# Layer 0: the softmax denominators divide the head outputs instead of the probabilities

## The chip, the cores and the metric

The kernel runs on one core of a Trainium2 chip. Its time is the device time of one execution in microseconds (us). The kernel before took 1253.75 us, the median of 3 runs (1253.59 to 1255.1).

The engines are named as the profile names them: PE is the matrix engine (PEld its weight loads), DVE the vector engine, ACT the scalar engine, POOL GpSimd, and SP the engine whose queue issues every DMA of this kernel. SBUF is the memory on the core, PSUM the matrix engine's result memory, DRAM the memory outside.

## The reference

Two layers over 1024 tokens of width 1024, with a final norm. Layer 0 has three groups of heads of width 64, all from one projection: A (6 heads, a window of 128 tokens on each side, a bias and a sink), B (6 heads, dense, with normalised and rotated q and k) and X (4 heads, attention to 256 memory tokens). Cut to what the change touches:

```python
def windowed_gqa_sink(q, k, v, sink, table):        # A
    ...
    sink_col = jnp.broadcast_to(sink.astype(jnp.float32).reshape(1, 1, KVH, G, 1, 1),
                                logits.shape[:-1] + (1,))
    p = jax.nn.softmax(jnp.concatenate([logits, sink_col], axis=-1), axis=-1)[..., :-1]
    out = jnp.einsum("bnkgqs,bnskd->bnqkgd", p.astype(v.dtype), vw)
...
    s = jnp.einsum("bqkgd,bskd->bkgqs", qi, k).astype(jnp.float32) * (D ** -0.5)     # B
    p = jax.nn.softmax(s, axis=-1)
    return jnp.einsum("bkgqs,bskd->bqkgd", p.astype(v.dtype), v)
...
def even_layer(x, ...):                              # layer 0
    y = jnp.concatenate([y_a.reshape(Bn, S, -1), y_b.reshape(Bn, S, -1),
                         y_x.reshape(Bn, S, -1)], axis=-1) * jax.nn.silu(gate)
    return x + y @ w_out
```

Layer 1 has the same shape with 6 differential heads (each the difference of two softmaxes, 128 wide) and 4 X heads; the change leaves its attention alone.

## The kernel before

**Work and its order.** Everything is computed in fp32 split into two parts of a narrower type, a high part (`wh`, `h`, `PTh`) and a low one (`wl`, `PTl`), so one product takes two or three matmuls. A scheduler places the instructions on each engine when the program is built; it fills the matrix engine's time between attention steps with pieces of the projections (line 297, the "jobs"). At run time each engine, and SP with its DMAs, runs its list in that fixed order and waits at each instruction for what it needs.

**An attention step** in layer 0 handles 128 query tokens of a head (B), 256 of a head in two blocks (A), or 128 of all four heads (X). There are 8 X steps, then 8 B steps of head 0, then 40 B and 24 A steps mixed by the string `PAT`. A step has these parts, spread over some five turns of `run_steps`:

1. `s1`: scores into a PSUM tile of tag S, which has two buffers (`sx`, `sb`, `sa`; line 509). DVE takes the minimum `mn` (negated scores), ACT writes `e` = exp and, by accumulation, its row sum `z`. For B a tiny DVE product `mr` = mn times rq (line 1063) stands between. For A, DVE adds the bias and takes the minimum in one instruction (line 1132), and ACT makes the sink's term `es` (line 1139), which DVE adds to `z` (line 1141).
2. `finish`: DVE takes 1/z (lines 596, 1067, 1143) and `e` is multiplied by it: on POOL for B (line 1068) and A (line 1149), on ACT for X (line 598).
3. `hop`, one turn later: a DMA copies `e` to `er`, the type that the matrix engine takes.
4. `s2`, two or three turns after `s1` (`ABLAG` is 3 for the mixed steps): PE transposes `er` into PSUM tiles of tag T, two buffers (`te`, `ta`); ACT writes the high part `PTh` (line 315), DVE the low part `PTl` (line 316), and that frees the T buffer.
5. `s3`, once for two B or X steps and once for an A step: the product with v (`ob`, `oa`, `ox`), in a PSUM tile of tag A, two buffers that the jobs' `acc` share. The high and low halves of v stand in the two halves of the 128 output partitions, so `y_evac` (lines 433 to 439) copies one half with ACT, adds with DVE (`yt`), and POOL multiplies the sum into the gate's tile `gy` at the head's 64 partitions.

When a gate tile is complete it is stored to DRAM (`ysc`). **The output projection** (`out_proj`, after the attention of each layer) goes over 8 token tiles in the order `ORD[l]`. `PRE` says for which tiles a part of the 8 terms was summed during the attention (layer 0: 4 of 8 for tiles 2 to 5, 6 of 8 for 6 and 7; layer 1: 6 of 8 for tiles 2, 3 and 4), so that these tiles are short here: a tile with all terms takes 48 matmuls, with 4 left 24, with 2 left 12. `pieces` gives each tile a buffer of tag S, and the last tile buffers of tag A. The first two tiles in the order begin before the last terms are there. After a tile's matmuls, DVE adds the residual (`x`, line 1274), ACT squares and sums, POOL makes the inverse root (line 229), DVE scales (`xs`, line 1295); in layer 0 PE transposes the result (`tx`, line 344) for layer 1's projections, whose first job needs tokens 0 to 511.

## Time and profile before

| | |
|---|---|
| median of the runs | 1253.75 us (1253.59 to 1255.1) |
| the profiled execution's own time | 1255.58 us |
| its span, first to last instruction | 1253.8 us |
| PE busy in the span | 1205.5 us (96%) |
| DVE, ACT, POOL busy | 817.1, 640.2, 413.5 us |
| mean busy share of the 16 DMA engines | 47.4% (the SP queue) |

By the timeline, layer 0's X steps lie at about 78 to 160 us, its other attention steps up to about 530 us, its output projection from 530 to 597 us, layer 1 after that, and layer 1's output projection from 1184 us to the end. The B steps of head 0 and the mixed steps overlap the projection jobs.

How to read the views: a row of grouped instructions gives line, engine, operation, output<-inputs, shapes, count, then busy us and mean ns, then the idle time of that engine just before these instructions and what ended it. A row of waits gives who waited for whom, total us, times, the longest. A row of windows gives a stretch of the span, its length, and each engine's busy us with its count of instructions, then the granted clock of the matrix engine (1.00 is full), the DMA engines' share and GB/s. Matmuls are pipelined, so PE's "busy" is an upper bound of its work.

### The profile page before, as it was taken

How to read it: one execution, taken by the hardware profiler on the slowest of the kernel's cores; microseconds unless marked ns; L12 is line 12 of the kernel's file. 1: busy time of each engine (PE TensorE's matmuls, PEld its weight loads, DVE VectorE, ACT ScalarE, POOL GpSimd, SP SyncE). 2: the span in 40 equal slices, each digit the busy share in tenths (PEclk: the TensorE clock that was granted, in tenths of full speed). 3: DMA queues.
4: the chain of work that ended last, by engine and by line, in shares of the span. 5: the costliest groups of instructions: out<-in, count | busy, mean ns of one | idle time of the engine just before them, and what ended most of it. 6: DMA issues, size and time to landing. Idle time of an engine off the chain costs nothing. (4 is left out here: it accounts for less than half of the span.)

```text
span 1253.8 us, 19637 instructions
## 1 busy us (share of the span) xinstructions
PE 1205.5 (96%) x6806; PEld 999.2 (80%) x6806; DVE 817.1 (65%) x1545; ACT 640.2 (51%) x1395; POOL 413.5 (33%) x390
## 2 busy tenths in 40 slices
PE   5999999999998999998999999999999999999997
PEld 4887788888887787887888778788887878877876
DVE  5547666377778788746355865766667666678444
ACT  6249654256666766533157644444444454456322
POOL 5023456266666565403122212212122131223100
PEclk9999999999999999999999999999999999999999
DMA  6654444545365575466644334243342433445363
GB/s 252 198 187 149 155 168 150 171 155 201 148 224 191 210 246 186 154 203 213 185 163 144 125 107 120 93 143 108 105 137 76 136 115 118 144 151 189 129 211 118
DMA packets 96350, 199.90 MB, mean 159 GB/s; under 512 B 11478, under 2 KB 31190, under 8 KB 96252
## 3 DMA queue, kind: packets, MB, share of 16 engines
q1 hardware_dynamic: 96252, 198.65, 47.4%
q8 instruction: 54, 0.88, 0.3%
q14 instruction: 44, 0.36, 0.1%
HBM read 79.32 MB, written 31.47 MB: 88 GB/s over the span
## 5 line engine op out<-in xcount | busy, mean ns | idle before, releaser
L297 PE MATMUL acc<-h,wh 128*128 128x512 f32 x1536 | 499.1, 399 | 7.3 <-DVE yt L624 3.1
L297 PEld LDWEIGHTS acc<-h,wh 128*128 128x128 f32 x1536 | 283.2, 188 | 73.3 <-issue 13.4
L297 PE MATMUL acc<-h,wl 128*128 128x512 f32 x768 | 304.6, 397 | 1.8 <-POOL wl L241 1.8
L241 POOL TENSOR_TENSOR wl<-wr,wh 128x512 fp32r<-128x512 f32 x96 | 124.9, 1302 | 340.0 <-DVE wh L239 125.2
L316 DVE TENSOR_TENSOR PTl<-te,PTh 128x512 fp32r<-128x512 f32 x224 | 148.2, 687 | 131.2 <-ACT PTh L315 128.4
L1440 ACT ACTIVATE e<-e,mn 128x1024 f32<-128x1024 f32 x96 | 110.2, 1149 | 130.7 <-DVE mn L1437 127.5
L297 PEld LDWEIGHTS acc<-h,wl 128*128 128x128 f32 x768 | 144.8, 189 | 35.5 <-issue 4.4
L315 ACT CAST PTh<-te 128x512 fp32r<-128x512 f32 x224 | 124.9, 591 | 30.2 <-PE te L540 24.6
L1068 POOL TENSOR_TENSOR e<-e,rz 128x1024 f32<-128x1024 f32 x48 | 91.7, 1913 | 78.1 <-DVE rz L1067 66.7
L1437 DVE CUSTOM_DVE_ANT_0 e<-sc,toep 128x1024 f32<-128x1024 f32 x96 | 113.9, 1217 | 5.3 <-PE sc L1431 5.0
L540 PEld LDWEIGHTS te<-identr,er 128*128 128x128 f32 x896 | 91.8, 143 | 21.1 <-issue 4.1
L540 PE MATMUL te<-identr,er 128*128 128x128 f32 x896 | 100.0, 246 | 7.5 <-issue 3.2
L239 DVE CAST wh<-wr 128x512 fp32r<-128x512 f32 x112 | 59.1, 530 | 43.9 <-PE acc L297 14.4
L1064 ACT ACTIVATE e<-sb,mr,nrq 128x1024 f32<-128x1024 f32 x48 | 58.0, 1208 | 48.4 <-DVE mr L1063 33.9
L1449 DVE SCALAR_TENSOR_TENSOR e<-e,mr 128x1024 f32<-128x1024 f32 x48 | 76.2, 1588 | 1.3
L1464 PE MATMUL oc<-PTh,v 128*128 128x256 f32 x384 | 74.8, 288 | 0.3 <-DVE ckl L1333 0.3
L660 PE MATMUL po<-woh,yh 128*128 128x512 f32 (+1 forms) x172 | 65.9, 383 | 1.5 <-DVE x L1274 1.5
L660 PE MATMUL po<-woh,yl 128*128 128x512 f32 (+1 forms) x172 | 65.6, 381 | 0.0
L660 PE MATMUL po<-wol,yh 128*128 128x512 f32 (+1 forms) x172 | 65.5, 381 | 0.0
L1464 PEld LDWEIGHTS oc<-PTh,v 128*128 128x128 f32 x384 | 61.5, 192 | 0.7 <-DVE ckl L1333 0.6
L1059 DVE TENSOR_REDUCE mn<-sb 128x1 f32<-128x1024 f32 x48 | 58.4, 1216 | 5.1 <-PE sb L509 4.7
L318 ACT ACTIVATE yh<-yr 128x256 fp32r<-128x256 f32 (+2 forms) x56 | 24.0, 448 | 67.3 <-DMA yr<-ysc 38.5
(199 smaller groups left out, 2247.1 us busy)
## 6 DMA issues: line engine op xcount, KB each, us to landing
er<-e SPq DMA_DIRECT2D x112, 512.0 KB, 2.9
wr<-in_w_in SPq DMA_DIRECT2D x96, 256.0 KB, 2.8
ysc<-gy SPq DMA_DIRECT2D x16, 512.0 KB, 2.9
wor<-in_w_out SPq DMA_DIRECT2D x32, 256.0 KB, 3.5
cq<-sg SPq DMA_DIRECT2D x64, 128.0 KB, 2.6
ck<-sg SPq DMA_DIRECT2D x48, 128.0 KB, 2.3
er<-e SPq DMA_DIRECT2D x12, 384.0 KB, 2.8
xpsc<-xh SPq DMA_DIRECT2D x18, 256.0 KB, 2.5
```

The source lines that it names most:

```text
L239: nc.vector.tensor_copy(hi, raw)
L241: (nc.vector if fast else nc.gpsimd).tensor_tensor(out=lo, in0=raw, in1=hi, op=ALU.subtract)
L297: lastmm[0] = nc.tensor.matmul(acc, a, b[:, k, c0:c0 + n], start=(i == 0), stop=(i == 23))
L315: nc.scalar.copy(hi, src)
L316: return nc.vector.tensor_tensor(out=lo, in0=src, in1=hi, op=ALU.subtract)
L540: nc.tensor.transpose(to[:, i * P:(i + 1) * P], e[0][:, k * P:(k + 1) * P], idt)
L660: lastmm[0] = nc.tensor.matmul(acc, a, b, start=(start and n == 0), stop=(stop and n == 2))
L1068: nc.gpsimd.tensor_tensor(out=et, in0=et, in1=rz.to_broadcast([P, 1024]), op=ALU.mult)
L1437: nc.vector.tensor_tensor_reduce(out=et, in0=Sp, in1=toeps[h][:, w0:w0 + 1024], scale=1.0, scalar=BIG, op0=ALU.add, op1=ALU.min, accum_out ...
L1440: nc.scalar.activation(et, et, AF.Exp, bias=mn[:, m:m + 1], scale=-1.0, accum_out=z[:, m:m + 1])
L1449: nc.vector.scalar_tensor_tensor(out=es[0], in0=es[1], scalar=c, in1=es[0], op0=ALU.mult, op1=ALU.add)
L1464: nc.tensor.matmul(acc, V[:, kt, v, :], pt[:, kt, :], start=(n == 0), stop=(n == 23))
```

## The change

- **Layer 0's probabilities stay undivided.** `finish` is gone for all three groups; `e` goes into the copy `er` as exp left it. The row sums of a pair of steps (B: two columns, X: eight) or of an A step (two) are kept in one tile.
- **1/z is spread by two DMAs.** In the hop, `z_rows` takes the reciprocal in place on DVE and a DMA writes it to DRAM with tokens along the row (`rz_d`; 256 single elements for A and B, 1024 for X). In `s2`, `z_tile` issues a second DMA that reads such a row into 64 partitions (`rzb`, 64 x 256, two buffers); X has four of these for a pair.
- **The gate's tile takes the factor.** POOL multiplies `rzb` into `gy` (64 x 256 in `y_evac`, 128 x 256 for X) before it multiplies the head output in.
- **The sink is a score column.** In A, ACT writes the sink's negated score into one more column beside each block's scores, and exp covers it, so that `z` holds it; `es` and its addition go. The copied tile is 769 or 641 columns wide.
- **`mr` moves from DVE to ACT** in the B steps.
- **The output projections** take their tiles in other orders (`ORD`), and the third tile in the order has two PSUM buffers of tag A instead of one of tag S (`pieces`). In both layers two more DVE, ACT and SP instructions come of that third tile's two halves.

Counted over the program, DVE has 94 instructions fewer, POOL 40 fewer, ACT 24 more, SP 118 DMAs more (116 for `rz_d` and `rzb`); PE has as many as before.

DVE at two B steps in the mixed part, before (`sb` are the scores, `wol` a piece of the output weights, `yt` a head output):

```order
L1059 TENSOR_REDUCE mn_4528<-sb_4523 128x1
L258 TENSOR_TENSOR wol_4545<-wor_4608,woh_4544 128x512
L1063 TENSOR_TENSOR mr_4532<-mn_4528,rq_81 128x1
L258 TENSOR_TENSOR wol_4545<-wor_4662,woh_4544 128x512
L438 TENSOR_TENSOR yt_4557<-oa_4550,yt_4557 64x256
L1067 RECIPROCAL rz_4579<-z_4531 128x1
L1059 TENSOR_REDUCE mn_4593<-sb_4588 128x1
L316 TENSOR_TENSOR PTl_4563<-te_4565,PTh_4561 128x4x128
L316 TENSOR_TENSOR PTl_4564<-te_4572,PTh_4562 128x4x128
L1063 TENSOR_TENSOR mr_4597<-mn_4593,rq_81 128x1
```

The same two steps on DVE now:

```order
L1096 TENSOR_REDUCE mn_4501<-sb_4496 128x1
L258 TENSOR_TENSOR wol_4518<-wor_4578,woh_4517 128x512
L439 TENSOR_TENSOR yt_4531<-oa_4523,yt_4531 64x256
L316 TENSOR_TENSOR PTl_4537<-te_4539,PTh_4535 128x4x128
L316 TENSOR_TENSOR PTl_4538<-te_4546,PTh_4536 128x4x128
L1096 TENSOR_REDUCE mn_4564<-sb_4559 128x1
```

`mr` and the reciprocal are gone from between; one reciprocal of both columns follows some rows later.

SP a little later in the mixed part, before (`er` of 1024 columns belong to B steps, of 768 and 640 to A steps; `wor` are output weights):

```order
L175 DMA er_4772<-e_4718 128x1024
L175 DMA wor_4994<-in_w_out0 128x512
L175 DMA er_4823<-e_4781 128x1024
L175 DMA er_4890<-e_4826 128x768
L175 DMA wor_5037<-in_w_out0 128x512
L175 DMA ysc0_94<-gy_3169 128x1024
```

The same steps on SP now:

```order
L175 DMA er_4742<-e_4690 128x1024
L175 DMA yr_4955<-ysc0_94 128x4x128
L175 DMA er_4791<-e_4751 128x1024
L175 DMA rz_d_4794<-es_4691 128x2x1
L175 DMA rz_d_4861<-z2_4799 128x2x1
L175 DMA er_4858<-e_4797 128x769
L175 DMA ysc0_94<-gy_3146 128x1024
L175 DMA wor_4962<-in_w_out0 128x512
L175 DMA rzb_4966<-rz_d_4794 64x256
L175 DMA wor_4982<-in_w_out0 128x512
L175 DMA er_4930<-e_4872 128x1024
```

Each `rzb`, which waits until its `rz_d` has landed, stands some four DMAs behind it, with `er` copies of later steps behind the `rzb`.

DVE in layer 1's output projection, where the first tiles end (`x1` is a tile's sum with the residual, `yl` the low part of a later tile's input), before:

```order
L1274 TENSOR_TENSOR x1_13081<-po_12974,xr_13060 128x1024
L319 SCALAR_TENSOR_TENSOR yl_13135<-yr_13133,yh_13134 128x512
L1274 TENSOR_TENSOR x1_13109<-po_13017,xr_13062 128x1024
L1283 TENSOR_SCALAR v_13086<-z4_13083 128x1
L319 SCALAR_TENSOR_TENSOR yl_13141<-yr_13139,yh_13140 128x256
L1295 SCALAR_TENSOR_TENSOR xs_13082<-x1_13081,r_13088,gb_12936 128x1024
L1283 TENSOR_SCALAR v_13114<-z4_13111 128x1
L319 SCALAR_TENSOR_TENSOR yl_13141<-yr_13139,yh_13140 128x128 x2
L1295 SCALAR_TENSOR_TENSOR xs_13110<-x1_13109,r_13116,gb_12936 128x1024
L1274 TENSOR_TENSOR x1_13153<-po_13120,xr_13079 128x1024
```

The same stretch now:

```order
L319 SCALAR_TENSOR_TENSOR yl_13052<-yr_13050,yh_13051 128x512
L319 SCALAR_TENSOR_TENSOR yl_13058<-yr_13056,yh_13057 128x256
L319 SCALAR_TENSOR_TENSOR yl_13058<-yr_13056,yh_13057 128x128 x2
L1316 TENSOR_TENSOR x1_13070<-po_12954,xr_13040 128x1024
L319 SCALAR_TENSOR_TENSOR yl_13089<-yr_13087,yh_13088 128x128 x2
L1316 TENSOR_TENSOR x1_13098<-po_12997,xr_13042 128x1024
L319 SCALAR_TENSOR_TENSOR yl_13161<-yr_13159,yh_13160 128x512
L1325 TENSOR_SCALAR v_13075<-z4_13072 128x1
L1337 SCALAR_TENSOR_TENSOR xs_13071<-x1_13070,r_13077,gb_12916 128x1024
L1325 TENSOR_SCALAR v_13103<-z4_13100 128x1
L1337 SCALAR_TENSOR_TENSOR xs_13099<-x1_13098,r_13105,gb_12916 128x1024
L1316 TENSOR_TENSOR x1_13179<-po_13109,xr_13068 128x512
```

Third in the order is now the full tile 5, whose input is split ahead of the first tile's sum; before it was tile 4, with 12 matmuls.

The diff, cut to its core:

```diff
--- before.py
+++ after.py
@@ -31,7 +31,7 @@
 FAST = ("m0", "m1", "m2", "m3")
-ORD = ((0, 1, 2, 3, 4, 5, 6, 7), (0, 1, 4, 2, 5, 3, 6, 7))
+ORD = ((0, 1, 2, 6, 3, 7, 4, 5), (0, 1, 5, 2, 6, 3, 4, 7))
 JORD = "xq0 m0 g6 m1 m2 g7 m3 bk bq0 bv bq1 g3 bq2 ak av aq0 g0 aq1 g4 g1 aq2 g5 g2".split()
...
@@ -430,8 +430,9 @@
-    def y_evac(M, acc, gt, hr, c0, n=256):
+    def y_evac(M, acc, gt, hr, c0, rzb, n=256):
         a = slice(hr * 64, hr * 64 + 64)
+        nc.gpsimd.tensor_tensor(out=gt[a, c0:c0 + n], in0=rzb[a, :n], in1=gt[a, c0:c0 + n], op=ALU.mult)
         b = slice(64 - hr * 64, 128 - hr * 64)
...
@@ -504,6 +505,22 @@
+
+    def z_rows(z, n):
+        nc.vector.reciprocal(z, z)
+        d = dr.tile([n, P], F32, name="rz_d")
+        dma(d.rearrange("n p -> p n"), z)
+        return d
+
+    def z_tile(M, d, parts):
+        t = M.at.tile([P, 256], F32, tag="rzb", name="rzb", bufs=2)
+        for rows, h in parts:
+            dma(t[rows, :], d[2 * h:2 * h + 2, :].rearrange("t p -> (t p)").partition_broadcast(64))
+        return t
+
+    def half_rows(hr):
+        return slice(hr * 64, hr * 64 + 64)
+
     def qk(ps_ap, qt, qc, kh, kl, ks, n):
...
@@ -587,10 +604,18 @@
                 ev = et.rearrange("p (h m) -> p h m", h=4)
-                z = stat("z4", 4)
+                if ydst == 0:
+                    if qb % 2 == 0:
+                        grp["z"] = stat("r8", 8, 2)
+                    z = grp["z"][:, qb % 2::2]
+                else:
+                    z = stat("z4", 4)
                 for h in range(4):
...
                                          scale=-1.0, accum_out=z[:, h:h + 1])
+                if ydst == 0:
+                    e[0] = et
+                    return None
                 def finish():
...
@@ -599,9 +624,19 @@
             st.s1 = s1
-            st.hop = word_copy(M, e)
-            st.s2 = dense_s2(M, e, st)
+            copy, turn = word_copy(M, e), dense_s2(M, e, st)
+            st.hop, st.s2 = copy, turn
             if st.sub == 1:
+                def hop(grp=grp, copy=copy):
+                    copy()
+                    grp["d"] = z_rows(grp["z"], 8)
+
+                def s2(grp=grp, turn=turn):
+                    grp["rzb"] = [z_tile(M, grp["d"], [(half_rows(j), XPOS[2 * p + j]) for j in range(2)]) for p in range(2)]
+                    return turn()
+                if ydst == 0:
+                    st.hop, st.s2 = hop, s2
+
                 def s3(qb=qb, grp=grp, ps=(0,)):
...
@@ -624,6 +659,8 @@
                         g = gates[6 + p][:, (qb - 1) * P:(qb + 1) * P]
+                        if ydst == 0:
+                            nc.gpsimd.tensor_tensor(out=g, in0=grp["rzb"][p], in1=g, op=ALU.mult)
                         nc.gpsimd.tensor_tensor(out=g, in0=t, in1=g, op=ALU.mult)
...
@@ -1058,20 +1095,26 @@
                 et = new_e(M)
-                z = stat("z")
+                if qb % 2 == 0:
+                    grp["z"] = stat("es", 2)
+                z = grp["z"][:, qb % 2:qb % 2 + 1]
                 mr = stat("mr")
-                nc.vector.tensor_tensor(out=mr, in0=mn, in1=rq[:, qb, h:h + 1], op=ALU.mult)
+                nc.scalar.activation(mr, mn, AF.Identity, scale=rq[:, qb, h:h + 1])
                 nc.scalar.activation(et, Sp, AF.Exp, bias=mr, scale=nrq[:, qb, h:h + 1], accum_out=z)
-                def finish():
-                    rz = stat("rz")
-                    nc.vector.reciprocal(rz, z)
-                    nc.gpsimd.tensor_tensor(out=et, in0=et, in1=rz.to_broadcast([P, 1024]), op=ALU.mult)
-                    e[0] = et
-                return finish
+                e[0] = et
             st.s1 = s1
-            st.hop = word_copy(M, e)
-            st.s2 = dense_s2(M, e, st)
+            copy, turn = word_copy(M, e), dense_s2(M, e, st)
+            st.hop, st.s2 = copy, turn
             if st.sub == 1:
+                def hop(grp=grp):
+                    copy()
+                    grp["d"] = z_rows(grp["z"], 2)
+
+                def s2(h=h, grp=grp):
+                    grp["rzb"] = z_tile(M, grp["d"], [(half_rows(h % 2), 0)])
+                    return turn()
+                st.hop, st.s2 = hop, s2
+
                 def s3(h=h, qb=qb, grp=grp):
...
@@ -1081,7 +1124,7 @@
                             n += 1
-                    y_evac(M, acc, gates[3 + h // 2], h % 2, (qb - 1) * P)
+                    y_evac(M, acc, gates[3 + h // 2], h % 2, (qb - 1) * P, grp["rzb"])
                     if h % 2 == 1 and qb == 7:
...
@@ -1113,16 +1156,22 @@
-            def s1(h=h, p=p, e=e):
+            def s1(h=h, p=p, e=e, grp=grp):
                 if p == 1 and h < 5:
...
                 Sp = ps_s("sa").rearrange("p (j c) -> p j c", j=2)
-                et = new_e(M)[:, :768].rearrange("p (j c) -> p j c", j=2)
+                et = new_e(M)[:, :770].rearrange("p (j c) -> p j c", j=2)
                 mn = stat("mn2", 2)
                 z = stat("z2", 2)
+                ends = [(min(8, qb + 2) - qb + 1) * P for qb in (2 * p, 2 * p + 1)]
+                if ends[0] == ends[1]:
+                    nc.scalar.copy(et[:, :, ends[0]], nsink[:, h:h + 1].to_broadcast([P, 2]))
+                else:
+                    for j in range(2):
+                        nc.scalar.copy(et[:, j, ends[j]:ends[j] + 1], nsink[:, h:h + 1])
                 for j in range(2):
...
@@ -1133,33 +1182,23 @@
                                                    accum_out=mn[:, j:j + 1])
-                    nc.scalar.activation(et[:, j, c:c + n], et[:, j, c:c + n], AF.Exp,
+                    nc.scalar.activation(et[:, j, c:c + n + 1], et[:, j, c:c + n + 1], AF.Exp,
                                          bias=mn[:, j:j + 1], scale=-1.0, accum_out=z[:, j:j + 1])
-                es = stat("es", 2)
-                nc.scalar.activation(es, mn, AF.Exp, bias=sinkb[:, h:h + 1], scale=1.0)
...
+                grp["z"] = z
+                e[0] = et
             st.s1 = s1
-            def hop(p=p, e=e):
-                t = M.at.tile([P, 1024], F32R, tag="er", name="er", bufs=M.cfg["er"])[:, :768]
-                a, b = (P if p == 0 else 0), (768 - P if p == 3 else 768)
+            def hop(p=p, e=e, grp=grp):
+                t = M.at.tile([P, 1024], F32R, tag="er", name="er", bufs=M.cfg["er"])[:, :770]
+                a, b = (P if p == 0 else 0), (769 - P if p == 3 else 769)
                 ef = e[0].rearrange("p j c -> p (j c)")
...
                 e[0] = t.rearrange("p (j c) -> p j c", j=2)
+                grp["d"] = z_rows(grp["z"], 2)
             st.hop = hop
...
+            def s2(h=h, p=p, e=e, grp=grp):
+                grp["rzb"] = z_tile(M, grp["d"], [(half_rows(h % 2), 0)])
                 ph, pl_ = grp["pt"] = [M.at.tile([P, 4, 256], F32R, tag="PT%s%d" % (c, p % 2), name="PTa", bufs=1)
...
@@ -1228,6 +1267,9 @@
         def pieces(i):
+            if i == 2:
+                p = [(ps_a("po")[:, 0:512], c, 512) for c in (0, 512)]
+                return p, p
             if i < TT - 1:
```

More of the change, by code (lines that the diff above doesn't have):

```diff
@@ L578, in x_steps, with s1 @@
             st.fill = fill
-            def s1(qb=qb, e=e):
+            def s1(qb=qb, e=e, grp=grp):
                 kh, kl = X["kh"], X["kl"]
@@ L1042, in b_step, with s1 @@
             e = [None]
-            def s1(h=h, qb=qb, e=e):
+            def s1(h=h, qb=qb, e=e, grp=grp):
                 if qb == 2 and h < 5:
@@ L1190, in s3 @@
                         n += 1
-                y_evac(M, acc, gates[h // 2], h % 2, p * 256)
+                y_evac(M, acc, gates[h // 2], h % 2, p * 256, grp["rzb"])
                 if h % 2 == 1 and p == 3:
```

13 lines of the change are left out of this document (removed).

## The prediction

> **What bounds the kernel now.** I read the page's engine shares first, then windows by stage, then PE's waits in these windows.
>
> ```profile
> PE 1205.5 (96%) x6806; PEld 999.2 (80%) x6806; DVE 817.1 (65%) x1545; ACT 640.2 (51%) x1395; POOL 413.5 (33%) x390
> ...
> 95.00:165.00 70.00, 65.00 (x380) 55.02 (x379) 47.35 (x84) 52.45 (x127) 29.26 (x24) 0.98 0.44 147
> 250.00:530.00 280.00, 269.26 (x1670) 229.83 (x1668) 216.83 (x482) 182.79 (x410) 168.09 (x153) 0.99 0.54 192
> 530.00:600.00 70.00, 65.88 (x321) 53.77 (x321) 40.11 (x65) 23.59 (x50) 14.59 (x18) 1.00 0.67 209
> 1184.00:1254.00 70.00, 61.84 (x294) 51.43 (x292) 28.48 (x52) 17.12 (x41) 5.82 (x9) 0.97 0.49 165
> ```
>
> PE is the bound, and the change leaves its 6806 instructions. So all that can be won is PE's idle time in the stages touched: 70 - 65.0 = 5.0 us around the X steps, 280 - 269.3 = 10.7 us in the mixed B and A steps, 70 - 65.9 = 4.1 us in layer 0's output projection, and in layer 1's what a wait holds. What PE waited for there, in this order of stages:
>
> ```profile
> PE acc L297 <- DVE yt L624: 3.1, 2, 1.8
> ...
> PE te L540 <- issue: 3.2, 5, 1.4
> PE sa L509 <- ACT e L1064: 2.1, 2, 1.1
> PE sa L509 <- DVE mn L1132: 1.7, 3, 1.1
> PE pre L660 <- DVE yt L438: 1.2, 1, 1.2
> PE te L540 <- DVE PTl L316: 0.9, 3, 0.4
> ...
> PE tx L344 <- DVE h L316: 1.7, 1, 1.7
> PE tx L344 <- DVE xs L1295: 1.2, 2, 0.7
> PE acc L297 <- DVE v L1283: 1.1, 1, 1.1
> ...
> PE po L660 <- DVE x L1274: 1.5, 1, 1.5
> ```
>
> These are waits for PSUM buffers that DVE or ACT empty late: tag A behind `yt`, tag S behind `e` and `mn`, tag T behind the splits. POOL's products and the `er` copies end none of them: two copies and the transposes that read them show why.
>
> ```profile
> 415.38 0.46 SPq L175 DMA_DIRECT2D er<-e  x1
> 425.04 0.84 PE L540 MATMUL te<-identr,er 128*128 128x128 f32 x8
> ...
> 448.43 0.47 SPq L175 DMA_DIRECT2D er<-e  x1
> 452.36 0.47 PE L540 MATMUL te<-identr,er 128*128 128x128 f32 x4
> ...
> er<-e SPq DMA_DIRECT2D x112, 512.0 KB, 2.9
> ```
>
> With 2.9 us from issue to landing (the last row, the page's median for `er`) the first lies ready 425.04 - 415.38 - 2.9 = 6.8 us before its use, the second, in the tightest stretch, 1.0 us. So taking 1.9 us of POOL out ahead of the copy wins nothing by itself; it makes cushion. The gain has to come from DVE and ACT.
>
> **The change, part by part.** The rows of what goes, and of the nearest to what comes:
>
> ```profile
> L598 ACT ACTIVATE e<-e,rz 128x256 f32<-128x256 f32 x64 | 28.4, 502 | 4.0 <-DVE rz L596 3.9
> L1063 DVE TENSOR_TENSOR mr<-mn,rq 128x1 f32<-128x1 f32 x48 | 9.3, 193 | 0.7
> L1067 DVE RECIPROCAL rz<-z 128x1 f32<-128x1 f32 x48 | 7.8, 162 | 30.5 <-ACT e L1064 30.4
> L1141 DVE TENSOR_TENSOR z<-z,es 128x2 f32<-128x2 f32 x24 | 6.9, 286 | 14.0 <-ACT es L1139 13.9
> L1139 ACT ACTIVATE es<-mn,small 128x2 f32<-128x2 f32 x24 | 6.8, 281 | 0.0
> L1483 ACT ACTIVATE z<-ssqc,es 128x1 f32<-128x1 f32 x48 | 10.0, 258 | 4.5 <-PE ssqc L1479 4.3
> L1068 POOL TENSOR_TENSOR e<-e,rz 128x1024 f32<-128x1024 f32 x48 | 91.7, 1913 | 78.1 <-DVE rz L1067 66.7
> L1149 POOL TENSOR_TENSOR e<-e,rz 128x384 f32<-128x384 f32 x36 | 29.7, 839 | 19.9 <-ACT yt L437 6.0 <-DVE rz L1143 6.0 <-ACT es L1139 4.5
> L1440 ACT ACTIVATION_READ_ACCUMULATOR e<-e,mn 128x1 f32 x96 | 17.9, 186 | 0.0
> L439 POOL TENSOR_TENSOR gy<-yt,gy 64x256 f32<-64x256 f32 x48 | 35.6, 742 | 21.2 <-DVE yt L438 19.9
> ```
>
> *X steps.* Half of the 64 scalings at line 598 are layer 0's: 32 x 0.502 = 16.1 us leave ACT, which has 52.5 of these 70 us. PE's 3.1 us are two waits for a tag A buffer, emptied by an ACT copy and then DVE; ACT has no backlog of scalings before the copy now. I take 2.5 us of the 3.1. Bounds: 0 (the copy still stands behind exps) and 3.1.
>
> *Mixed steps, DVE.* 48 x 0.193 (`mr`), 24 x 0.286 (sink) and, with the X steps' 8, 80 reciprocals go; 52 come: about 9.3 + 6.9 + 28 x 0.16 = 20.7 us less. More weighs that DVE stood idle 30.5 us ahead of line 1067 and 14.0 us ahead of line 1141, waiting for an exp just issued, with splits queued behind. The reciprocal now comes a turn later, so most of that wait goes; what is late next on DVE is the split, for PE's next transposes.
>
> *Mixed steps, ACT.* 48 `mr` at the 258 ns of the nearest row (line 1483, also one column with a factor) add 12.4 us; 24 `es` go (6.8 us) and 30 sink copies come (at most 30 x 0.281 = 8.4 us, at least 30 x 0.186, the mere read of an accumulator at line 1440). ACT rises from 182.8 to about 197 of 280 us, and each B step's exp has a small one before it; in exchange the exp no longer waits for a DVE product that had queued behind a weight split.
>
> *Mixed steps, sum.* The listed waits of this stage are 3.2 + 2.1 + 1.7 + 1.2 + 0.9 = 9.1 us. DVE gets looser by far more than ACT gets tighter: I take half, 4.5 us. Bounds: 9.1 above; below, -12.4 us, all of `mr` on the path.
>
> *POOL.* 91.7 us at line 1068 and at least 29.7 at line 1149 (36 of its 48) go, 56 x 0.742 = 41.6 come: some 80 us less, no PE wait hangs on it, 0. Behind a product that waits for `rzb` stand the weight splits `wl`, and PE waits for these; POOL's free time is the cover, and without it one late `rzb` would cost PE what it is late.
>
> *SP.* Its issues in 350 to 500 us, and the DMAs nearest to the new ones:
>
> ```profile
> L175 SPq DMA_DIRECT2D er<-e x33: 464/470/492, 355.4 to 497.6; - x33
> L175 SPq DMA_DIRECT2D wor<-in_w_out x16: 327/340/722, 361.3 to 438.2; - x16
> L175 SPq DMA_DIRECT2D xh<-in_x x11: 332/510/1837, 396.2 to 494.3; - x11
> L175 SPq DMA_DIRECT2D yr<-ysc x10: 370/382/585, 398.7 to 491.0; - x10
> L175 SPq DMA_DIRECT2D aq_d<-sg x8: 470/591/716, 352.2 to 366.3; - x8
> L175 SPq DMA_DIRECT2D xpsc<-xh x8: 320/326/542, 432.9 to 488.6; - x8
> ...
> xkl<-xkl SPq DMA_DIRECT2D x8, 64.0 KB, 2.0
> skew_d<-vec_d SPq DMA_DIRECT2D x6, 256.0 KB, 5.9
> ```
>
> At the medians these are 15.5 + 5.4 + 5.6 + 3.8 + 4.7 + 2.6 = 37.6 of 150 us. The 33 steps there bring about 23 pairs of `rz_d` and `rzb`, 46 issues of 0.47 = 21.6 us, and 23 waits for an `rz_d` to land. No DMA of single elements is in the trace: its landing lies between 2.0 us (the smallest copies) and 5.9 us (a small DRAM row spread to 128 rows). I take some 2.5, nearer to the first, since it moves 1 KB; other issues stand between the two, so 1 to 2 us of waiting is left. 37.6 + 21.6 + 23 x 1.5 = 94 of 150 us: it fits, and the `er` behind have gained the 1.9 us of POOL. In the tight stretch I charge 1.0 us.
>
> *Layer 0's output projection.* The waits are 1.7, 1.2 and 1.1 us, at the end where two short tiles (12 matmuls, 2.5 us at the window's 65.88 / 321 = 0.205) follow each other faster than DVE ends a tile. Now short ones stand between long ones; the 8 transposes of the last but one tile (0.84 us, as the row of eight `te` above) lie where `acc` waited 1.1. I take 2.0. Bounds 0 and 4.0.
>
> *Layer 1's output projection.* PE waited 1.5 us for a tag S buffer after three quick tiles; the third tile now has tag A buffers and 48 matmuls. I take 1.5; bounds 0 and 1.5.
>
> *Clock.* Two windows that hold idle PE time show a reduced clock:
>
> ```profile
> 100.00:150.00 50.00, 46.21 (x273) 39.13 (x271) 33.28 (x59) 41.75 (x107) 19.85 (x18) 0.97 0.52 169
> 400.00:450.00 50.00, 44.44 (x270) 37.61 (x270) 40.90 (x85) 34.86 (x75) 30.79 (x26) 0.97 0.66 225
> ```
>
> 0.03 x 50 = 1.5 us each. I count 0; 3.0 is the upper bound if less idling spares them. The Trainium skill ("TensorE: Matmul & The Clock Gate", Part 1: The HAM clock gate) has the clock halved after about 3.4 us of an idle window. The trace disagrees in part: the longest single wait there is 1.8 us, and the clock fell. By the page neither dip hangs on these short waits and the sum gets 0; by the rows it could get 3.0.
>
> *Sum.* 2.5 + 4.5 - 1.0 + 2.0 + 1.5 = 9.5 us. The profiled execution took 1255.6 us, so it would take 1246.1; it is 1.8 us above the median of the runs, and from that median 1253.75 - 9.5 = **1244.3 us**.
>
> **The rivals.**
>
> *Only the edges win.* ACT takes DVE's place as what PE waits for in the mixed steps, so that X and the two projections alone give 2.5 + 2.0 + 1.5 = 6.0 us: 1247.8. For it: ACT's rise; against: 45 us of DVE standing idle for exps.
>
> *Nothing that can be measured.* PE is busy 96%, and a wait taken from one place reappears at the next, as the order on PE is another now: 1 to 2 us off, 1252.5.
>
> *Slower: `mr` on ACT's path.* ACT runs in order; if each B step's exp, and with it the tag S buffer, comes 0.258 us later, 48 x 0.258 = 12.4 us are lost against the 6.0 won: 1260.2. It decides from 6.0 / 0.258 = 23 of the 48 steps on. Against it: `mr` left DVE, where it cost 0.193 in the same chain, so the net is nearer 0.07 a step.
>
> *Slower: SP.* If `rzb` holds SP for w us each, SP is full from w = (150 - 37.6 - 21.6) / 23 = 3.9; with a landing of 5.9 less one issue, w = 5.4, PE loses (5.4 - 3.9) x 48 = 72 us at worst, and at w = 4.2 some 14 us, which with 9.5 won gives 1258. The Trainium skill ("DMA: Bandwidth & Descriptors", Rules for kernel authors) speaks for it: a last dimension that is not contiguous becomes one descriptor per element, and a transpose by a plain DMA is put 19 times behind the hardware's. No run here shows such a DMA; by that rule this rival's time would hold, by the rows the forecast's.
>
> **How the numbers follow.** Forecast 0.54 (1244.3; its own range 1239 to 1249), edges only 0.18 (1247.8), nothing 0.13 (1252.5), `mr` 0.09 (1260), SP 0.06 (1258 and more). About 0.2% (2.5 us) can be told from no change; so faster 0.72, same 0.13, slower 0.15. The upper bounds added, 3.1 + 9.1 + 4.0 + 1.5 + 3.0 = 20.7 us, would give 1233; that all are reached is unlikely, and I set the low end at 1237. The high end of 1254.5 takes in "nothing" and leaves out the two slower ones.
>
> **What would show it.** Right: no PE wait on `yt` L624 around the X steps; waits of `te` and `sa` between 250 and 530 us at half; PE's idle time in 530 to 600 us near 2 us; no `po` wait on `x` in layer 1; `er` still landed some us before `te`. Wrong: PE waits on ACT's `e` or `PTh` of more than before ("`mr`"); SP waiting on `rz_d` for over 3 us each and `te` on `er` ("SP"); POOL standing on `rzb` with `acc` waiting on `wl`. The forecast falls if PE's idle time in 250 to 530 us stays near 10.7 us.

## The result and the profile after

The changed kernel takes **1413.09 us** (median of 4 runs, 1412.32 to 1413.56); the kernel before took 1253.67 us beside it. The ratio is 1.1278, 95% interval 1.1261 to 1.1295. The forecast was 1244.3 us, range 1237.0 to 1254.5.

The page's engine shares after:

```profile
PE 1250.9 (89%) x6806; PEld 1032.7 (73%) x6806; DVE 798.0 (57%) x1451; ACT 639.7 (45%) x1421; POOL 326.4 (23%) x350
```

Windows of the profile after, three of them the stretches that the prediction shows (stretch, length, busy us of PE, PEld, DVE, ACT and POOL with their counts, granted clock, DMA share, GB/s):

```profile
95.00:165.00 70.00, 52.41 (x287) 43.71 (x285) 34.84 (x59) 38.06 (x98) 22.42 (x21) 0.88 0.64 135
250.00:530.00 280.00, 217.17 (x1199) 184.84 (x1197) 135.60 (x266) 129.21 (x301) 69.73 (x79) 0.88 0.58 141
530.00:600.00 70.00, 46.27 (x246) 38.38 (x246) 34.07 (x69) 33.20 (x80) 16.04 (x19) 0.79 0.73 152
760.00:1410.00 650.00, 637.41 (x3544) 519.98 (x3542) 417.20 (x737) 303.68 (x656) 130.94 (x132) 1.00 0.41 133
```

The span grew from 1253.8 to 1410.5 us, by 156.7. PE's idle time in it is 1410.5 - 1250.9 = 159.6 us where it was 48.3, so 111.3 us more; its busy time is 45.4 us longer for the same 6806 instructions, because the granted clock fell to 0.79 to 0.88 in the three windows where PE now idles. Nearly all of it lies in layer 0's attention: from 760 us on the clock is 1.00 and PE is busy 98%. DVE's and POOL's work fell about as forecast (by 19.1 and 87.1 us; 20.7 and some 80 were forecast), and that is worth nothing here.

What was waited for between 78 and 700 us of the span (who, for whom, total us, times, longest):

```profile
PE sa L526 <- DVE mn L1181: 46.9, 14, 7.9
PE te L557 <- DMA er<-e: 19.1, 6, 9.9
PE ob L1124 <- ACT PTh L315: 15.9, 2, 12.8
PE pre L697 <- DVE yt L439: 10.2, 1, 10.2
...
POOL gy L435 <- DMA rzb<-rz_d: 256.6, 38, 13.9
ACT e L1171 <- DMA er<-e: 38.7, 7, 11.7
DVE e L1181 <- DMA er<-e: 30.5, 9, 8.1
```

PE waits for `mn` (line 1181), and DVE's line 1181 and ACT's line 1171, which fill an `e` tile of the next A step, wait for an `er` copy: an `e` tile is free for the next step only when the copy has read it. So the `er` copies are late, at both of their ends. SP's own waits show what stands ahead of them:

```profile
SPq L175 <- DMA rz_d<-es: 140.1, 24, 8.9
SPq L175 <- DMA rz_d<-z: 70.6, 16, 9.0
SPq L175 <- DMA rz_d<-r: 16.9, 4, 7.4
```

And the page's DMA issues (count, KB each, median us from issue to landing):

```profile
er<-e SPq DMA_DIRECT2D x112, 512.0 KB, 3.3
er<-e SPq DMA_DIRECT2D x12, 384.5 KB, 6.9
rzb<-rz_d SPq DMA_DIRECT2D x64, 64.0 KB, 3.7
rz_d<-es SPq DMA_DIRECT2D x24, 1.0 KB, 9.5
rz_d<-z SPq DMA_DIRECT2D x24, 1.0 KB, 9.0
```

An `rz_d` of 1 KB lands 9.0 to 9.5 us after its issue; the prediction took 2.5 and gave 5.9 as the upper end. SP stands 140.1 + 70.6 + 16.9 = 227.6 us waiting for it. The `er` copies of some A steps (384.5 KB) take 6.9 us where they took 2.8.

At this point the obvious reading is: SP waits, and the copies queue behind it. It is mostly wrong, as the next section shows.

### The profile page after: what moved, and what is told of

The parts are those of the page before. It is cut to its first block, busy times and chain, and to the rows that moved or that the text cites. A ratio compares the mean times of both kernels' runs of the same rounds, so it can differ in the third digit from the quotient of the medians.

```text
span 1410.5 us, 19702 instructions
## 1 busy us (share of the span) xinstructions
PE 1250.9 (89%) x6806; PEld 1032.7 (73%) x6806; DVE 798.0 (57%) x1451; ACT 639.7 (45%) x1421; POOL 326.4 (23%) x350
## 5 line engine op out<-in xcount | busy, mean ns | idle before, releaser
L297 PE MATMUL acc<-h,wh 128*128 128x512 f32 x1536 | 505.2, 403 | 3.2 <-DVE wh L239 1.5
L297 PEld LDWEIGHTS acc<-h,wh 128*128 128x128 f32 x1536 | 286.8, 191 | 71.3 <-issue 12.2
L297 PE MATMUL acc<-h,wl 128*128 128x512 f32 x768 | 307.8, 401 | 0.9 <-POOL wl L241 0.9
L557 PE MATMUL te<-identr,er 128*128 128x128 f32 x896 | 100.8, 249 | 27.7 <-DMA er<-e 19.1
L435 POOL TENSOR_TENSOR gy<-rzb,gy 64x256 f32<-64x256 f32 x48 | 35.5, 740 | 262.3 <-DMA rzb<-rz_d 256.6
L239 DVE CAST wh<-wr 128x512 fp32r<-128x512 f32 x112 | 54.8, 491 | 65.9 <-DMA wr<-in_w_in 24.0
L1124 PE MATMUL ob<-PTh,v 128*128 128x256 f32 x192 | 56.6, 321 | 15.9 <-ACT PTh L315 15.9
L697 PE MATMUL po<-woh,yl 128*128 128x512 f32 (+1 forms) x172 | 66.7, 388 | 0.0
L526 PE MATMUL sa<-ak,q 128*128 128x384 f32 (+1 forms) x48 | 22.2, 462 | 50.0 <-DVE mn L1181 46.9
## 6 DMA issues: line engine op xcount, KB each, us to landing
er<-e SPq DMA_DIRECT2D x12, 384.5 KB, 6.9
```

Of the source, the lines that this page charges most:

```text
L297: lastmm[0] = nc.tensor.matmul(acc, a, b[:, k, c0:c0 + n], start=(i == 0), stop=(i == 23))
L557: nc.tensor.transpose(to[:, i * P:(i + 1) * P], e[0][:, k * P:(k + 1) * P], idt)
L697: lastmm[0] = nc.tensor.matmul(acc, a, b, start=(start and n == 0), stop=(stop and n == 2))
```

## The experiments

Four readings stood against each other: **WAIT** (SP stands for each `rz_d`, and the copies behind it are issued late), **TRAFFIC** (the single elements keep the DMA engines from other work, whether SP waits or not), **ORDER** (not the DMAs, but the new order on PE, DVE and ACT, `mr` on ACT included), and later two readings of what makes a single element slow: **LINE** (where in DRAM it is written) and **COUNT** (a write of 4 bytes is slow wherever it goes). **BLOCK**, in the later expectations, is TRAFFIC as it stood after experiment 1. The diffs are cut to their core. Every ratio is to runs of the kernel before that were taken beside the experiment; their medians lie between 1253.7 and 1254.9 us.

**1. The wait taken away, the elements kept.**

```diff
     dma(d.rearrange("n p -> p n"), z)
-    return d
+    return A["odd_norm"][0].rearrange("(n p) -> n p", p=P)
```

> The changed kernel, but each rzb copy reads a row of an input instead of the rz_d it belongs to, so that nothing waits for an rz_d; all rz_d are still written, element by element, and as many DMAs are issued. It leaves out the division itself (the gate takes another factor). Theory WAIT (SP stands for each rz_d to land, about 9 us from issue, and the er copies queue behind it): the loss of 159 us goes, 1240 to 1262 us, SP's waits for rz_d gone. Rival TRAFFIC (16384 single elements keep the DMA engines busy, so that all copies land late): stays above 1350 us, er landing late as before. Rival ORDER (the loss has nothing to do with the DMAs, but with the order on PE, DVE and ACT that the undivided probabilities and mr on ACT bring): stays near 1413 us.

Measured: 1386.7 us, ratio to before 1.1064 (1.1036 to 1.1091). SP's waits for `rz_d` are down to 22.7 us, and 26 of the 159 us are gone. SP's wait for the B steps' `rz_d`, the mixed steps' window, and the waits for copies:

```profile
SPq L175 <- DMA rz_d<-es: 18.6, 7, 3.9
```

```profile
250.00:530.00 280.00, 227.71 (x1260) 195.13 (x1258) 145.48 (x282) 137.31 (x319) 81.33 (x93) 0.89 0.70 152
```

```profile
POOL gy L435 <- DMA rzb<-in_odd_norm: 95.1, 24, 16.0
DVE e L1181 <- DMA er<-e: 43.2, 8, 13.9
ACT e L1171 <- DMA er<-e: 41.7, 9, 8.9
```

WAIT falls as the main cause: hardly anything waits for the element writes any more, yet the `er` copies are no earlier than in the changed kernel, and even `rzb`, which reads a row that was there from the start, is waited for up to 16.0 us. Something holds the DMA engines. Their packets show it: between 250 and 530 us a packet of 4 KB takes 0.159 us in the median, here and in the kernel before, but the longest took 7.2 us here against 0.9 before, and 2.4% took over 1 us where none did before.

**2. The wait kept, the single elements taken away.**

```diff
-    dma(d.rearrange("n p -> p n"), z)
+    dma(d, src[:n, P:2 * P])        # whole rows of 128 elements of the step's e
```

> The changed kernel, but rz_d is written as whole rows of 128 elements (2 or 8 rows of the step's e), not as 256 or 1024 single elements; rzb waits for it as before. It leaves out the division itself. WAIT with single elements as the cause of the late landing: rz_d lands within 2 to 3 us, SP waits some 56 x 1 us, 1245 to 1275 us. TRAFFIC: the same, 1245 to 1275. If the wait for any rz_d, of whatever form, is the cause (two DMAs in a chain): rz_d's landing stays near 9 us and the time near 1400. ORDER: near 1413.

Measured: 1247.89 us, ratio 0.9949 (0.9934 to 0.9964). As many DMAs, the same chain from `rz_d` to `rzb`, the same order of engines; only the form of one kilobyte is another, and the 159 us are gone and 6 more. SP's wait for `rz_d` is still in the program, and it is short:

```profile
SPq L175 <- DMA rz_d<-e: 7.9, 6, 2.2
```

ORDER falls, and a chain of two DMAs is no cause by itself.

**3. The two DMAs alone, put into the kernel before.**

```diff
     copy()
+    grp["d"] = z_rows(grp["rz"], 2)      # 256 single elements to DRAM
 ...
+    z_tile(M, grp["d"], [(half_rows(h % 2), 0)])     # read back, used by nobody
     return turn()
```

> The kernel before, with the two DMAs added and nothing else: after each pair's or A step's copy an rz_d of as many single elements (of 1/z, which the kernel has anyway), in s2 the rzb that reads it; rzb is used by nobody, the probabilities are divided as before. Computes the reference in full. WAIT: the whole loss or most of it, 1370 to 1440 us, with the waits of SP for rz_d at 200 us or more. TRAFFIC: the same. ORDER: 1254 to 1265, the DMAs alone cost nothing much.

Measured: 1457.33 us, ratio 1.1616 (1.1581 to 1.1651), above the expected 1370 to 1440.

```profile
SPq L175 <- DMA rz_d<-rz: 280.6, 46, 10.9
```

The DMAs alone make the whole loss, and more than in the change. A likely reason, not tested, is that the change has more cushion: the probabilities here wait for POOL's product before they are copied.

**4. The rest of the change, without the DMAs.** Division on POOL and ACT as before; sink column, `mr` on ACT, both `ORD` and the third tile's buffers as changed. Against the changed kernel:

```diff
+    def finish():
+        rz = stat("rz")
+        nc.vector.reciprocal(rz, z)
+        nc.gpsimd.tensor_tensor(out=et, in0=et, in1=rz.to_broadcast([P, 1024]), op=ALU.mult)
-    grp["d"] = z_rows(grp["z"], 2)
-    grp["rzb"] = z_tile(M, grp["d"], [(half_rows(h % 2), 0)])
```

> All the rest of the change without the spread: the probabilities are divided where the kernel before does it (POOL for A and B, ACT for X), with the sink as a score column, mr on ACT, both ORD and the third tile's two buffers as changed. Computes the reference in full. WAIT and TRAFFIC: no loss is left, 1246 to 1256 us (the forecast's 2.0 + 1.5 us of the output projections won, the mixed steps within some us either way). ORDER: near 1413 if the order or mr on ACT is the cause; near 1254 if it is the undivided probabilities.

Measured: 1250.42 us, ratio 0.9973 (0.9954 to 0.9991). Nothing in this part of the change loses time, and in experiment 2 the undivided probabilities don't either.

**What the trace says of one such write.** SP's timeline of the changed kernel around two of them (start, us, engine, line, operation):

```profile
273.45 0.50 SPq L175 DMA_DIRECT2D er<-e  x1
274.00 0.58 SPq L175 DMA_DIRECT2D rz_d<-es  x1
275.93 0.47 SPq L175 DMA_DIRECT2D er<-e  x1
276.50 0.54 SPq L175 DMA_DIRECT2D rz_d<-z  x1
282.83 0.48 SPq L175 DMA_DIRECT2D rzb<-rz_d  x1
```

Each of these DMAs raises its semaphore 16 times. The times of the 16 increments, in us of the span, taken from the same trace:

```
rz_d issued 274.00: 279.57 280.23 280.61 280.62 280.97 281.23 281.35 281.47 281.58 281.98 282.00 282.17 282.21 282.38 282.41 282.81
er   issued 275.93: 279.75 280.41 280.77 280.80 281.16 281.39 281.53 281.64 281.76 282.19 282.22 282.34 282.40 282.56 282.62 283.00
rz_d issued 276.50: 281.51 281.78 282.55 282.88 282.93 282.94 283.35 283.36 283.46 283.79 283.89 283.90 284.25 284.41 284.42 284.67
```

The `er` copy between the two is one of 320.5 KB. Such a copy landed 2.4 us after its issue in the kernel before (the median on its page), which would be at 278.3. Its own data packets are on time: they start between 277.1 and 278.0 and end by 278.1. But its increments follow those of the `rz_d` ahead of it one by one, each about 0.2 us later (both lists are in order of time; the records don't name the DMA engine). Another `rz_d`, issued at 175.16 us 0.9 us behind an `er` copy, had nothing issued behind it until it landed at 184.53. In the DMA records its 4-byte packets all start by 177.4 us, at 9 ns each. So the elements are not slow to fetch; their writes are slow to be confirmed, and what lies behind is confirmed only after them. The Trainium skill ("DMA: Bandwidth & Descriptors", Queues, rings and completion order) has it that a DMA's semaphore increment lands only after every earlier write of that DMA engine has landed. The trace agrees: 0.2 us behind, 16 times over. That fits with how little it helped to take SP's wait away. Once even a copy ahead was touched: of the `er` copy issued 0.9 us before the `rz_d` at 175.16, 15 increments came by 177.13 us and the last at 183.02. Why isn't known.

The medians of the 16 increments over all these DMAs between 70 and 750 us of the span, in us after the end of the issue, first, middle and last (in the records of experiment 1 some increments are missing, for X in two of four DMAs, so its row is rough by some tenths):

```
                       er of 512 KB and less   rz_d, 256 elements (B)   rz_d, 1024 elements (X)
before                 2.21  2.29  2.41        -                        -
changed                2.93  3.79  5.05        4.11  6.72  9.04         7.48  9.30  10.64
1  no wait             2.69  4.12  6.96        3.33  7.08  9.85         7.69  9.78  11.78
6  far (512 bytes)     2.26  2.39  2.85        1.82  1.94  2.31         2.79  3.32   3.73
7  near (64 bytes)     2.27  2.44  2.89        1.83  2.02  2.57         2.81  3.44   3.83
8  four per 64         2.28  2.49  3.09        1.88  2.34  3.40         3.03  4.04   4.69
```

Four times as many elements cost only some 2 us more in the changed kernel. That speaks against a price for each element. What the two forms have in common is that the elements lie side by side, sixteen in each 64 bytes and 128 in each row of 512.

**5. `rzb` later.** The read is issued at the product with v and multiplied in last.

```diff
-    def s2(h=h, grp=grp):
-        grp["rzb"] = z_tile(M, grp["d"], [(half_rows(h % 2), 0)])
-        return turn()
 ...
     def s3(h=h, qb=qb, grp=grp):
+        grp["rzb"] = z_tile(M, grp["d"], [(half_rows(h % 2), 0)])
```

> The changed kernel with rzb issued a turn or two later (in s3, at the product with v, and multiplied into the gate last). Computes the reference in full. Theory BLOCK, formed after the runs without the wait: the 256 single elements of one rz_d hold the DMA engines for some 7 us, and every copy that lies behind on the same engines waits, whether SP waits or not: 1370 to 1410 us, although SP's waits for rz_d fall from 228 us to under half. Theory WAIT: with the wait halved or gone half the loss or more goes, below 1330 us.

Measured: 1403.65 us, ratio 1.1190 (1.1158 to 1.1222). The time came out as expected of BLOCK, but by a weaker test than meant: SP's waits for `rz_d` fell only from 227.6 to 184.2 us, not under half. That WAIT is the smaller part rests on experiment 1.

**6, 7, 8. Where the elements go.** All three are experiment 1 with one thing more: the distance in DRAM from one element of `rz_d` to the next. The number of elements and of DMAs is that of experiment 1, and each of the four traces has 29591 packets of 4 bytes.

```diff
-    d = dr.tile([n, P], F32, name="rz_d")
-    dma(d.rearrange("n p -> p n"), z)
+    d = dr.tile([n, P, P], F32, name="rz_d")      # 512 bytes apart; [n, P, 16]: 64; [n, P, 4]: 16
+    dma(d[:, :, 0].rearrange("n p -> p n"), z)
```

> The kernel of the run without the wait (rzb reads an input row), with one thing more: in rz_d each element lies 512 bytes from the next instead of 4, so that no two writes go to the same 512 bytes; 256 or 1024 single elements are written as before. It leaves out the division itself. LINE (the single writes are slow because they go to the same short stretch of DRAM and follow one another there): 1245 to 1290 us, against 1386.7 with the elements side by side. COUNT (a write of 4 bytes to DRAM is slow wherever it goes): 1365 to 1405 us.

> As the run with far elements, but 64 bytes apart instead of 512 (rzb reads an input row, nothing waits for an rz_d; leaves out the division itself). If the writes get in each other's way only within 64 bytes: 1243 to 1262 us, rz_d's increments within 3 us as with 512. If the stretch in which they do is longer (up to 512 bytes): above 1300 us, between 1300 and 1390.

> As the runs with far and near elements, but 16 bytes apart, so that four writes fall into each 64 bytes instead of one (near) or sixteen (side by side). Leaves out the division itself. If writes to the same 64 bytes follow one another at some 0.43 us each (7 us / 16): 3 x 0.43 = 1.3 us on top of the near elements' landing of 2.4 us after issue, about 3.7 us, and 1245 to 1265 us, since an engine held so short has slack. If what counts is whether they share a stretch at all: landing near 9 us and above 1350 us.

Measured: 1245.66 us with 512 bytes (ratio 0.9931, 0.9903 to 0.9958), 1247.12 with 64 (0.9941, 0.9924 to 0.9959), 1253.36 with 16 (0.9983, 0.9968 to 0.9998), against 1386.7 with 4. The page's DMA issues of the far elements:

```profile
er<-e SPq DMA_DIRECT2D x112, 512.0 KB, 3.2
er<-e SPq DMA_DIRECT2D x12, 384.5 KB, 3.1
...
rz_d<-es SPq DMA_DIRECT2D x24, 1.0 KB, 3.1
rz_d<-z SPq DMA_DIRECT2D x24, 1.0 KB, 2.6
```

Their windows:

```profile
95.00:165.00 70.00, 67.39 (x399) 56.52 (x399) 45.70 (x78) 46.71 (x112) 25.71 (x25) 1.00 0.50 158
250.00:530.00 280.00, 274.42 (x1710) 235.73 (x1709) 200.85 (x409) 192.65 (x458) 91.93 (x109) 1.00 0.63 208
530.00:600.00 70.00, 67.08 (x319) 53.71 (x318) 40.28 (x66) 23.80 (x50) 13.26 (x16) 1.00 0.67 209
```

The mixed steps' window with four elements per 64 bytes (its profiled execution, 1257.74 us, was the slowest of its eight):

```profile
250.00:530.00 280.00, 269.67 (x1658) 232.05 (x1658) 196.25 (x399) 190.23 (x452) 88.94 (x106) 0.98 0.64 202
```

All three times lie in the range that the expectations gave if the place counts and not the number. 256 single elements have landed 2.1 to 2.6 us after the end of the issue when they lie 64 or 512 bytes apart, and after some 9 us when they lie side by side, with 16 bytes in between (3.1 to 3.4 us). Not the number of writes is dear, and not the 4 bytes, but writes of one DMA that lie close together in DRAM. A row of 128 values of 1/z is 512 bytes, and all 128 partitions write into it.

How long the stretch is in which such writes hold one another up isn't settled. No run has elements 8 or 32 bytes apart, and by the last increments of the B steps two prices fit about equally well. For each further write into the same 64 bytes it would be (9.85 - 2.57) / 15 = 0.49 us, so 1.5 us for the three of the run with 16 bytes, where 0.8 was measured. For each further write into the same 512 bytes it would be (9.85 - 2.31) / 127 = 0.06 us, so 1.8 us for the 31 of that run, where 1.1 was measured. Nor do the runs show why such writes follow one another (in the memory or on the way to it).

**9. The column turned into rows first.** DVE's transpose of 32 by 32 blocks makes stretches of 128 bytes of it, so that an A or B `rz_d` is 8 writes instead of 256. The tiles `zin` and `zout` take the place of two that the kernel only clears.

```diff
-    nc.vector.reciprocal(z, z)
+    nc.vector.reciprocal(zin[:, :n], z)
+    zo = zout.tile([P, 32], F32, tag="zo", name="zo", bufs=3)
+    nc.vector.transpose(zo, zin)
     d = dr.tile([n, P], F32, name="rz_d")
-    dma(d.rearrange("n p -> p n"), z)
+    for i in range(n):
+        dma(d[i].rearrange("(b c) -> b c", b=4), zo[i::32, :])
```

> The changed kernel, but DVE turns the column of 1/z into rows first (its transpose of blocks of 32 by 32), so that an rz_d is written as 8 stretches of 128 bytes (two DMAs of 4) instead of 256 elements; one DMA more for each pair or A step, one DVE instruction more; rzb waits for it as in the change. Computes the reference in full. BLOCK by number of elements: 1244 to 1258 us, as the run with whole rows (1247.9) plus the DMAs and DVE's work. If any write shorter than a row of 512 bytes holds the engines as long: rz_d lands after 6 us or more and the time is above 1300.

Measured: 1249.45 us, ratio 0.9962 (0.9950 to 0.9974): 0.4% faster than the kernel before, clear of 1 in its interval, with the change's idea intact. SP's wait for `rz_d`, and two windows:

```profile
SPq L175 <- DMA rz_d<-zo: 5.8, 9, 1.1
```

```profile
165.00:250.00 85.00, 85.00 (x443) 70.69 (x442) 41.84 (x69) 33.83 (x63) 33.14 (x32) 1.00 0.55 171
250.00:530.00 280.00, 275.19 (x1713) 236.22 (x1712) 208.91 (x453) 193.09 (x460) 94.65 (x111) 1.00 0.61 209
```

SP's waits for `rz_d` are 5.8 us in all, against 227.6.

**10, 11. On that version: `rzb` later, and `mr` back on DVE.**

> The run with short rows, with rzb issued later as in the run with the late rzb and multiplied into the gate last. Computes the reference in full. With the single elements gone SP's waits for rz_d are only 5.8 us in all, so the later issue should change little: 1246 to 1251 us against 1249.45. If SP's waits or POOL's wait for rzb still cost PE time: 1243 to 1246.

> The run with short rows, with mr back on DVE as in the kernel before. Computes the reference in full. If mr on ACT lies on the path of exp (the rival at 1260 us: 48 x 0.258 = 12.4 us, less DVE's 48 x 0.193 = 9.3): 1246 or less against 1249.45. If DVE was the later of the two, as the forecast has it: 1250 to 1254. Within 1 us: mr lies on no path.

```diff
-    nc.scalar.activation(mr, mn, AF.Identity, scale=rq[:, qb, h:h + 1])
+    nc.vector.tensor_tensor(out=mr, in0=mn, in1=rq[:, qb, h:h + 1], op=ALU.mult)
```

Measured: `rzb` later 1252.15 us, ratio 0.9976 (0.9962 to 0.9989), a little above the 1246 to 1251 expected and no gain; `mr` on DVE 1255.70 us, ratio 1.0001 (0.9985 to 1.0017), which is above the 1250 to 1254 of the forecast's reading and the opposite of the rival's. The windows of `mr` on DVE, against those of experiment 9 above:

```profile
165.00:250.00 85.00, 83.76 (x434) 69.80 (x435) 43.21 (x77) 32.88 (x59) 33.59 (x32) 1.00 0.52 164
250.00:530.00 280.00, 274.23 (x1706) 233.92 (x1705) 218.62 (x494) 184.25 (x421) 92.44 (x111) 1.00 0.61 208
```

PE is busy 1.2 us less in the first stretch (the B steps of head 0) and 1.0 us less in the second. That is 2.2 of the 4.4 us between the two spans (1247.7 and 1252.1); where the rest lies isn't settled.

**12. The output projections alone, in the kernel before.**

```diff
-ORD = ((0, 1, 2, 3, 4, 5, 6, 7), (0, 1, 4, 2, 5, 3, 6, 7))
+ORD = ((0, 1, 2, 6, 3, 7, 4, 5), (0, 1, 5, 2, 6, 3, 4, 7))
 ...
+    if i == 2:
+        p = [(ps_a("po")[:, 0:512], c, 512) for c in (0, 512)]
+        return p, p
```

> The kernel before with the output projections of the change alone (both ORD, the third tile's two buffers). Computes the reference in full. The forecast's terms: 2.0 us in layer 0's and 1.5 in layer 1's, 1250.2 us. If a wait taken there reappears at the next tile: 1252.5 to 1255.

Measured: 1250.78 us, ratio 0.9969 (0.9957 to 0.9981), so 3.9 us less (2.4 to 5.4) where the forecast had 2.0 + 1.5. The windows of both projections:

```profile
530.00:600.00 70.00, 66.72 (x324) 54.39 (x323) 39.85 (x66) 23.59 (x51) 14.00 (x17) 1.00 0.70 220
1184.00:1254.00 70.00, 60.36 (x289) 50.80 (x288) 28.68 (x54) 17.42 (x43) 5.11 (x9) 0.97 0.49 165
```

In layer 0's projection PE is busy 66.7 of 70 us instead of 65.9. In layer 1's it idles 6.2 us up to the end of the span at 1250.6 us, where it idled 8.0 up to 1253.8.

## Why the prediction was wrong

**The step that failed** is the price of the new DMA in the paragraph on SP: "its landing lies between 2.0 us ... and 5.9 us", of which 2.5 was taken because it moves 1 KB. The measured landing is 9.0 to 9.5 us (the page's medians, from the start of the issue). The bounds came from rows whose DMAs write contiguous stretches (1 and 2 KB a row). None of them writes elements side by side from 128 partitions, and so none bounded this one from above, however the prediction put it.

**The second half of the failure is the place of the cost.** The rival on SP had the right DMA and the right row to watch (SP waiting over 3 us each for `rz_d`; it was 227.6 / 44 = 5.2 us), but it priced it by SP's time alone: 1258 us, 72 us at worst. What it left out is that the copies behind are held on the DMA engines too. In numbers, with the wait taken away first: from the changed kernel to experiment 1, SP's wait is worth 1413.1 - 1386.7 = 26.4 us; from there to the far elements, the writes side by side are worth 1386.7 - 1245.7 = 141.0 us; and the rest of the change wins 1253.7 - 1245.7 = 8.0 us. 26.4 + 141.0 - 8.0 = 159.4, the measured loss. The 8.0 is 9.2 against the kernel before beside that run, so this split is good to about 1 us. It also depends on the order: with the writes made quick and SP's wait kept (experiments 2 and 9) the loss is gone whole, as SP then waits 7.9 and 5.8 us in all. So the part that the rival priced, SP's time, is a sixth of the loss, and its chance of 0.06, with a high end of 1254.5, was far too low for a DMA of a form that the trace of before didn't show. Both of its signs came: SP waited over 3 us each, and `te` waited on `er` (19.1 us).

The Trainium skill ("DMA: Bandwidth & Descriptors", Rules for kernel authors) was cited against the change: a last dimension that isn't contiguous becomes one descriptor per element and should be rearranged. The advice was right here, and the rival built on it came nearer than the forecast. Its reason isn't the one that decides: the far elements have as many single writes (29591 packets of 4 bytes in both traces) and lose nothing.

**PE's idle time is all there is to win**: this held, and the changed kernel shows what it means when something else breaks: 87 us less on POOL and 19 us less on DVE weigh nothing.

**The terms of the sum**, read in the far elements, where the stall is gone and the work is the change's own but for the rows that `rzb` reads (PE's busy us in the same windows, against before; the windows stand at fixed times and the far elements run ahead, so the work in them differs a little, and these are estimates):

- X steps: forecast 2.5, measured 67.39 - 65.00 = 2.4.
- Mixed steps: 4.5, measured 274.42 - 269.26 = 5.2.
- Layer 0's output projection: 2.0, measured 67.08 - 65.88 = 1.2 (0.8 in experiment 12).
- Both projections together: 3.5, measured 3.9 in experiment 12.
- Clock: 0 was counted, 3.0 the bound; in two of the three windows it was 0.98 and 0.99 and is 1.00 now. Part of the 3.0 was won.
- SP's ordinary waiting: 1.0 charged; with an `rz_d` that lands in time SP waits 5.8 us in all (experiment 9), and the mixed steps show no loss by it (PE busy 275.19 us there, 274.42 in the far elements).

The signs that the prediction named for its waits came in the far elements too. No PE wait on `yt` is left around the X steps, and none on `x` in layer 1. In 250 to 530 us PE idles 5.6 us instead of 10.7, and `te` and `sa` stand at 1.7 us instead of 7.9; one wait on ACT's `PTh` is new:

```profile
PE ob L1124 <- ACT PTh L315: 2.2, 1, 2.2
PE sa L526 <- DVE mn L1181: 1.1, 2, 0.7
PE te L557 <- DVE PTl L316: 0.6, 2, 0.4
```

Together the far elements take 1245.66 us against the forecast's 1244.3. That nearness is in part luck: there are two runs, and the interval of their gain is 5.3 to 12.2 us. That run also leaves the dependence out, so it isn't the change. With the dependence intact, and with 76 more DMAs and the transposes, experiment 9 wins 4.8 us, half of the forecast's 9.5. So the reading of PE's waits was sound in the main, and one term, the DMA, sank the forecast.

**`mr` on ACT's path** (the rival at 1260 us): wrong in sign, as far as the kernel of experiment 9 shows. With `mr` on DVE it becomes slower by 6 us, although `mr` on ACT took 0.295 us each (median) and not the 0.258 assumed. That is the direction of the forecast's "DVE gets looser by far more than ACT gets tighter".

**POOL**: that its 80 us buy nothing was right. The cover named for `rzb` was POOL's free time; POOL waited 256.6 us for `rzb`, the largest row among the new waits, and in experiment 1 that row fell to 95.1 us while the time fell by 2%. So it was mostly a symptom.

## What to carry to other kernels

A DMA whose form is not in the trace has no upper bound from rows of other forms, however few bytes it moves: price it by what it could hold up (the queue that issues it and the engines that carry it), and keep the range open on that side. Don't write a column of SBUF into a short contiguous row of DRAM element by element: make stretches of 128 bytes first, as DVE's transpose did here (1249.45 us), or put the elements 64 bytes apart if the reader can take it (1247.1 us, in a run whose reader took another row). And when a queue seems to stall on a wait, take the wait away and keep the work before believing it: here the largest waits in the page (POOL's and SP's) carried a sixth of the loss when they alone were taken away.

## What the runs showed of the hardware

- Single 4-byte writes of one DMA that lie close together in DRAM hold one another up. With 256 elements the last increment comes 8.6 to 9.9 us after the end of the issue when they lie 4 bytes apart, 3.1 to 3.4 at 16 bytes, 2.4 to 2.6 at 64 and 2.1 to 2.3 at 512 (medians of the A and B steps).
- While they do, copies of other tiles behind them on the same DMA engines aren't confirmed: the last of an `er` copy's 16 increments came 5.05 us after the end of the issue in the median of the changed kernel and 7.0 in experiment 1, up to 13.8, where it was 2.4.
- Writes of 128 bytes to DRAM, four per DMA, land 1.4 us after the end of the issue (median in experiment 9).
- An idling PE pays twice here: of 156.7 us of longer span, 111.3 are idle time and 45.4 are the same instructions at a granted clock that fell to 0.79 to 0.88 in the windows shown.
